# Six high and six low weight tiles, each at its own place in a 512-byte line

## The chip, the cores and the metric

The kernel runs on one core of a Trainium2 chip. The metric is the device time of one execution in microseconds (us); lower is better. A profile of one execution goes with it: its span runs from the first to the last instruction, and the execution's own time is a little longer.

## What is computed

A decoder trunk of two layers over 512 tokens of width 1024, in float32. Each layer is a half-step SwiGLU block, a mixer (a gated linear recurrence and a sliding-window attention side by side), and another half-step SwiGLU block:

```python
for l in range(DEPTH):                       # DEPTH = 2
    h = rms_norm(x, gn[0])
    x = x + 0.5 * rms_norm(swiglu(h, w_ffn1_gate[l], w_ffn1_up[l], w_ffn1_down[l]), gn[1])
    h = rms_norm(x, gn[2])
    proj = h @ w_in[l]                       # 1024 x 4864
    ...
    y_hg = hgrn2_mixer(hq, hf, hi, hg, ...) @ w_branch_hgrn[l]
    y_at = swa_sink_attention(aq, ak, av, attn_sinks[l]) @ w_branch_attn[l]
    mixed = sigmoid(gate_a) * y_hg + sigmoid(gate_b) * y_at
    x = x + rms_norm(mixed @ w_out[l], gn[3])
    h = rms_norm(x, gn[4])
    x = x + 0.5 * rms_norm(swiglu(h, w_ffn2_gate[l], w_ffn2_up[l], w_ffn2_down[l]), gn[5])
```

The feed-forward width is 2816. Nearly all of the arithmetic is in products of the 512 x 1024 activations with the weights, and each weight is used once.

## The kernel before

**Every product is done as three.** A float32 operand is kept as a pair: `hi`, its value rounded to the float32r type that the matrix engine takes in one pass, and `lo`, what the rounding left. `mm3` (L406) multiplies hi by hi, hi by lo and lo by hi into one accumulator. So three matmuls stand one behind the other: two with the high stationary operand, and one with the low one. The moving operand is 256 or 512 columns wide.

**The weight stream.** A weight unit is a tile of 128 partitions x 1024 columns, 4096 bytes in each partition. `load` (L235) brings it from HBM into one of four `w32` tiles. `split` (L322) and `quarter` (L255) make of it a high tile (`whi`, a rounding copy on ACT) and a low tile (`wlo`, a subtraction on DVE, or a negated copy on ACT to which a DMA issued by POOL adds the raw weight, L360). There are six tiles of each (`WS = 6`), used in turn. A consumer takes a tile in eight slices of 128 columns, which is 512 bytes of each partition.

**Who reads the tiles.** In the projections the weight slice is the stationary operand and the activations (tag `s`) move: the trace writes `acc<-s,whi` (output, moving, stationary). They are 512 wide in the mixer and in the first stages of a SwiGLU block, and 256 wide in `sevenths`, which makes the rest of gate and up with seven products in place of eight. In `down` it is the other way round: weight pieces move, 512 columns in four runs of 512 bytes, and activations are stationary (`acc<-whi,s`).

**What sets the order.** TensorE runs in the order in which the code is written; the other engines are ordered by a scheduler, with some steps pinned. A list of delays (`WAIT`) sets where the mixer's small steps are put between the matmuls.

**Where tiles lie.** All tiles of a tag are laid one behind the other in a partition, in the order in which tags first appear. As built, before the change, the starts of the tiles within a 512-byte line are these: all 61 `s` tiles at byte 64, all four `w32`, all six `whi` and all six `wlo` tiles at byte 128, `tt` and `m` (scratch of DVE and ACT) at byte 320, the identity matrix `ident` at byte 32, the matrix `ones` at byte 0. Tile sizes of these tags are multiples of 512 bytes, and so every slice of every such tile starts at the byte of its tag.

Of the kernel before, what the change touches and what calls it, by code (L numbers as in the profile page):

```python
# [8 lines left out]
F32R = mybir.dt.float32r  # L9
# [6 lines left out]
P = 128  # L16
D = 1024
# [19 lines left out]
W32, WS, AHEAD, TAIL, FIRST, EARLY, LATE = 4, 6, 3, 4, 7, 4, 8  # L37
# [7 lines left out]
def trunk(ctx: ExitStack, tc: tile.TileContext, xin, wall, gains, lbT, hgain, sinks, c_dist, c_mask, c_ident, out):  # L45
    nc = tc.nc
    cp = ctx.enter_context(tc.tile_pool(name="cp", bufs=1))
    sb = ctx.enter_context(tc.tile_pool(name="sb", bufs=1))
# [9 lines left out]
    def nm(s):  # L58
        seq[0] += 1
        return f"{s}_{seq[0]}"  # L60
# [3 lines left out]

    def small(shape, tag, bufs=4, dt=F32):
        return sb.tile(shape, dt, tag=tag, name=nm(tag), bufs=bufs)

    def acc():
        return ps.tile([P, S], F32, tag="acc", name=nm("acc"), bufs=5)
# [66 lines left out]
    eps_t = const([P, 1], "eps_t")  # L136
    nc.vector.memset(eps_t, EPS)
    nc.scalar.activation(out=small([P, 1], "warm", 2), in_=eps_t, func=AF.Copy, scale=eps_t)


# [15 lines left out]
    class Stream:  # L156
# [98 lines left out]
        def quarter(self, it):  # L255

            q, u, v, h = it.q, it.u, it.u + it.n, (slice(0, S), slice(S, D))

            def sums(o, x, y, op):
                for c in range(2):  # L260
                    pin(nc.vector.tensor_tensor(o[c], x[c], y[c], op=op))  # L261

            def raw(i):
                self.load(i + 1)
                return [self.raw[i][:, c] for c in h]

            def leave(i):
                self.raw.pop(i)
                self.freed += 1
                self.load(self.freed + W32)  # L270

            if it.kind in ("p1", "p2"):
                w = raw((u if it.kind == "p1" else v) + q)
            elif it.kind in ("p3", "p5"):
                w = self.b22[q]
            elif it.kind == "p7":

                w = self.b12[q]
                if q == 0:
                    sums(w, w, self.b22[q], ALU.add)  # L280
            else:
                w = self.b12[q]
            it.hi = sb.tile([P, D], F32R, tag="whi", name=nm("whi"), bufs=WS)
            it.lo = sb.tile([P, D], F32R, tag="wlo", name=nm("wlo"), bufs=WS)
            for c in range(2):
                i = nc.scalar.copy(it.hi[:, h[c]], w[c])  # L286
                if self.pinned:
                    pin(i)
            if it.kind == "p7" and q + 1 < it.n:
                sums(self.b12[q + 1], self.b12[q + 1], self.b22[q + 1], ALU.add)  # L290
            elif it.kind == "p6":
                sums(self.b22[q], self.b22[q], w, ALU.add)
            for c in range(2):
                pin(nc.vector.tensor_tensor(it.lo[:, h[c]], w[c], it.hi[:, h[c]].bitcast(F32), op=ALU.subtract))  # L294
            if it.kind == "p7":

                sums(w, raw(u + q), w, ALU.subtract)
                leave(u + q)
            elif it.kind == "p5":
                self.b22[q] = None  # L300
                if q + 1 < it.n:
                    sums(self.b12[q], raw(v + q), self.b12[q], ALU.add)
                    leave(v + q)
            elif it.kind == "p4":
                self.b12[q] = None
                if q == 0:
                    i = it.n - 1
                    sums(self.b12[i], raw(v + i), self.b12[i], ALU.add)
                    leave(v + i)
            self.done += 1  # L310
            self.flight += 1
# [10 lines left out]
        def split(self):  # L322
            it = self.items[self.done]
            if it.kind[0] == "p":
                return self.quarter(it)
            u, last = it.u, it.kind in "uvd"
            self.load(u + (1 if it.kind in "uv" else 2))
            it.hi = sb.tile([P, D], F32R, tag="whi", name=nm("whi"), bufs=WS)
            it.lo = sb.tile([P, D], F32R, tag="wlo", name=nm("wlo"), bufs=WS)
            w, h = self.raw[u], (slice(0, D // 2), slice(D // 2, D))  # L330
            cols = (slice(0, D),)
            if it.kind == "u" and u < 2:
                cols = h
            if it.kind in "bcd":
                v = self.raw[u + 1]
            if it.kind == "b":

                self.t13 = sb.tile([P, D], F32, tag="tt", name=nm("tt"), bufs=2)
                pin(nc.vector.tensor_tensor(self.t13[:, h[0]], w[:, h[0]], v[:, h[0]], op=ALU.add))
                pin(nc.vector.tensor_tensor(self.t13[:, h[1]], v[:, h[0]], v[:, h[1]], op=ALU.add))  # L340
                w = self.t13
                self.product()
            elif it.kind == "c":

                t = sb.tile([P, D], F32, tag="tt", name=nm("tt"), bufs=2)
                pin(nc.vector.tensor_tensor(t[:, h[0]], self.t13[:, h[0]], v[:, h[1]], op=ALU.add))
                pin(nc.vector.tensor_tensor(t[:, h[1]], t[:, h[0]], w[:, h[1]], op=ALU.add))  # L347
                w = t
            elif it.kind == "d":
                w = v  # L350
                cols = h[1:]
            for c in cols:
                i = nc.scalar.copy(it.hi[:, c], w[:, c])  # L353
                if u < 6 or self.pinned or self.tight:
                    pin(i)
                if it.kind in "vad":
                    i = nc.scalar.mul(it.lo[:, c], w[:, c], -1.0)  # L357
                    if self.pinned or self.tight:
                        pin(i)
                    nc.gpsimd.dma_start(it.lo[:, c].bitcast(F32), w[:, c], accum_op=ALU.add)  # L360
                else:
                    self.hold(nc.vector.tensor_tensor(it.lo[:, c], w[:, c], it.hi[:, c].bitcast(F32), op=ALU.subtract))  # L362
            self.done += 1
            self.flight += 1
            if last:
                nu = u + (1 if it.kind in "uv" else 2)
                for i in range(u, nu):
                    self.raw.pop(i)
                    self.freed += 1
                self.load(self.freed + W32)  # L370
# [93 lines left out]
    def rstd(sq, box, wait):  # L464


        n = sq.shape[-1] // P
        c = aux()
        for tt in range(n):
            mm(c[:, tt : tt + 1], sq[:, tt * P : (tt + 1) * P], ones[:, 0:1], True, True)  # L470
        rc = small([P, TT], "rc", 6)
        dg = big(F32, [P, TT, P])
        with tc.high_priority(offset=int(WAIT["first"])):
            nc.scalar.activation(out=rc[:, :n], in_=c[:, :n], func=AF.Sqrt, bias=eps_t, scale=1.0 / D)
            nc.vector.reciprocal(rc[:, :n], rc[:, :n])
            nc.vector.tensor_tensor(
                dg[:, :n, :], ident.unsqueeze(1).to_broadcast([P, n, P]),
                rc[:, :n].unsqueeze(2).to_broadcast([P, n, P]), op=ALU.mult,
            )
        yield WAIT[wait]  # L480
        b = aux()
        mm(b[:, : n * P], ones, dg[:, :n, :].rearrange("p a b -> p (a b)"), True, True)
        box.append(b)
# [15 lines left out]
    def pair_split(v, how=split):  # L499
        return how(v, to=(big(F32R, [P, 2, S // 2]), big(F32R, [P, 2, S // 2])))  # L500
# [139 lines left out]
    def root(ss, n):  # L640

        t = small([P, 2], "rt", 8)
        nc.vector.tensor_scalar(t[:, 0:1], ss[:, 0:1], 1.0 / n, EPS, op0=ALU.mult, op1=ALU.add)
        pin(nc.scalar.activation(out=t[:, 1:2], in_=ss[:, 1:2], func=AF.Sqrt, bias=t[:, 0:1], scale=1.0 / n))
        nc.vector.reciprocal(t[:, 1:2], t[:, 1:2])
        return t[:, 1:2]

    class Late:
# [20 lines left out]
        def first(self, k):  # L669
            x = big(F32R, [P, 2, S // 2])  # L670
            self.x1.append(split(self.src[k][:, HALF[0]], to=(x[:, 0, :], x[:, 1, :]), hold=pin))
# [973 lines left out]
```

## Time and profile before

| | |
|---|---|
| median of 3 runs | 2070.87 us (2067.01 to 2071.06) |
| the profiled execution's own time | 2067.36 us |
| its span | 2064.8 us |
| granted TensorE clock, mean | 0.999 |
| TensorE matmul busy | 2053.1 us, 99% |
| VectorE busy | 1629.0 us, 79% |
| ScalarE busy | 1249.3 us, 61% |
| GpSimd busy | 268.0 us, 13% |

Matmuls overlap: one begins before the one ahead of it has ended, and so its duration in the trace (276 ns for one of 256 columns) is longer than the distance to the next. What counts for the time is the distance from start to start, called cadence here. Where TensorE is busy without a break, the number of matmuls in a stretch gives it.

### The profile page before, as it was taken

How to read it: one execution, taken by the hardware profiler on the slowest of the kernel's cores; microseconds unless marked ns; L12 is line 12 of the kernel's file. 1: busy time of each engine (PE TensorE's matmuls, PEld its weight loads, DVE VectorE, ACT ScalarE, POOL GpSimd, SP SyncE). 2: the span in 40 equal slices, each digit the busy share in tenths (PEclk: the TensorE clock that was granted, in tenths of full speed). 3: DMA queues.
4: the chain of work that ended last, by engine and by line, in shares of the span. 5: the costliest groups of instructions: out<-in, count | busy, mean ns of one | idle time of the engine just before them, and what ended most of it. 6: DMA issues, size and time to landing. Idle time of an engine off the chain costs nothing. (4 is left out here: it accounts for less than half of the span.)

```text
span 2064.8 us, 36590 instructions
## 1 busy us (share of the span) xinstructions
PE 2053.1 (99%) x13571; PEld 1826.7 (88%) x13571; DVE 1629.0 (79%) x2910; ACT 1249.3 (61%) x2209; POOL 268.0 (13%) x318
## 2 busy tenths in 40 slices
PE   9999999999999999999999999999999999999999
PEld 8899978887888999997899998898778989999987
DVE  5887899666776778888988788977676758788888
ACT  7566687456355556658866666864653545666684
POOL 0111140000000011113201121400000100111140
PEclk9999999999999999999999999999999999999999
DMA  8587798312237367878758878872122562778794
GB/s 250 151 188 192 187 196 242 103 62 72 72 95 212 113 145 190 189 188 206 205 152 189 196 187 202 185 220 84 52 82 62 137 190 93 182 191 189 181 203 123
DMA packets 166802, 328.07 MB, mean 159 GB/s; under 512 B 19072, under 2 KB 85088, under 8 KB 166624
## 3 DMA queue, kind: packets, MB, share of 16 engines
q1 hardware_dynamic: 122416, 228.16, 33.1%
q0 software_dynamic: 44064, 97.54, 28.3%
q8 instruction: 106, 1.74, 0.3%
q14 instruction: 72, 0.59, 0.1%
q10 hardware_dynamic: 144, 0.05, 0.0%
HBM read 213.43 MB, written 14.73 MB: 110 GB/s over the span
## 5 line engine op out<-in xcount | busy, mean ns | idle before, releaser
L114 PE MATMUL acc<-s,whi 128*128 128x256 f32 (+1 forms) x4976 | 1031.0, 306 | 0.0
L114 PEld LDWEIGHTS acc<-s,whi 128*128 128x128 f32 x4976 | 793.8, 188 | 52.4 <-issue 3.2
L114 PE MATMUL acc<-s,wlo 128*128 128x256 f32 (+1 forms) x2488 | 759.9, 305 | 2.5 <-DMA wlo<-w 1.9
L114 PEld LDWEIGHTS acc<-s,wlo 128*128 128x128 f32 x2488 | 467.9, 188 | 30.7 <-DMA wlo<-w 4.4
L114 PE MATMUL acc<-whi,s 128*128 128x512 f32 x1360 | 446.6, 397 | 1.9 <-DVE s L432 1.3
L353 ACT CAST whi<-w 128x1024 fp32r<-128x1024 f32 (+1 forms) x310 | 286.8, 928 | 139.4 <-PE acc L114 90.0
L353 ACT CAST whi<-tt 128x1024 fp32r<-128x1024 f32 x160 | 167.9, 1049 | 252.3 <-DVE tt L347 171.4
L360 POOL DMA_DIRECT2D wlo<-w x178 | 154.2, 868 | 1249.5 <-ACT wlo L357 539.1
L114 PEld LDWEIGHTS acc<-whi,s 128*128 128x128 f32 x1360 | 255.7, 188 | 62.5 <-DVE s L432 2.2
L362 DVE TENSOR_TENSOR wlo<-tt,whi 128x1024 fp32r<-128x1024 f32 x160 | 196.0, 1225 | 135.7 <-ACT whi L353 129.8
L114 PE MATMUL acc<-wlo,s 128*128 128x512 f32 x680 | 267.6, 394 | 0.6 <-DVE wlo L294 0.6
L114 PE MATMUL aux<-s,whi 128*128 128x256 f32 (+1 forms) x1296 | 230.1, 280 | 0.0
L362 DVE TENSOR_TENSOR wlo<-w,whi 128x1024 fp32r<-128x1024 f32 (+1 forms) x132 | 157.5, 1204 | 78.7 <-ACT whi L353 77.8
L114 PEld LDWEIGHTS aux<-s,whi 128*128 128x128 f32 x1296 | 197.5, 188 | 1.1 <-issue 0.5
L114 PE MATMUL aux<-s,wlo 128*128 128x256 f32 (+1 forms) x648 | 181.0, 279 | 0.0
L114 PEld LDWEIGHTS acc<-wlo,s 128*128 128x128 f32 x680 | 128.0, 188 | 29.9 <-DVE wlo L294 2.4
L357 ACT ACTIVATE wlo<-w 128x1024 fp32r<-128x1024 f32 (+1 forms) x178 | 153.5, 863 | 0.2 <-PE acc L114 0.2
L114 PE MATMUL aux<-whi,s 128*128 128x512 f32 x432 | 145.3, 394 | 0.0
L443 POOL DMA_DIRECT2D s<-s x128 | 111.3, 969 | 217.5 <-ACT s L431 98.5
L114 PEld LDWEIGHTS aux<-s,wlo 128*128 128x128 f32 x648 | 121.6, 188 | 0.4
L294 DVE TENSOR_TENSOR wlo<-s,whi 128x512 fp32r<-128x512 f32 x160 | 102.5, 683 | 9.9 <-ACT whi L286 8.1
L431 ACT CAST s<-s 128x512 fp32r<-128x512 f32 (+1 forms) x140 | 70.6, 547 | 44.5 <-DVE s L490 41.0
(185 smaller groups left out, 2481.6 us busy)
## 6 DMA issues: line engine op xcount, KB each, us to landing
w<-wall SPq DMA_DIRECT2D x267, 512.0 KB, 4.1
wlo<-w POOLq DMA_DIRECT2D x98, 512.0 KB, 5.3
w<-wall SPq DMA_DIRECT2D x224, 128.0 KB, 3.5
wlo<-w POOLq DMA_DIRECT2D x80, 256.0 KB, 3.3
s<-wall SPq DMA_DIRECT2D x128, 128.0 KB, 4.4
s<-s POOLq DMA_DIRECT2D x64, 256.0 KB, 4.9
x_d<-s SPq DMA_DIRECT2D x48, 256.0 KB, 3.8
s<-x_d SPq DMA_DIRECT2D x48, 256.0 KB, 5.3
```

The costliest lines, as they stand in the source:

```text
L114: nc.tensor.matmul(o, lhsT, rhs, start=start, stop=stop)
L294: pin(nc.vector.tensor_tensor(it.lo[:, h[c]], w[c], it.hi[:, h[c]].bitcast(F32), op=ALU.subtract))
L353: i = nc.scalar.copy(it.hi[:, c], w[:, c])
L357: i = nc.scalar.mul(it.lo[:, c], w[:, c], -1.0)
L360: nc.gpsimd.dma_start(it.lo[:, c].bitcast(F32), w[:, c], accum_op=ALU.add)
L362: self.hold(nc.vector.tensor_tensor(it.lo[:, c], w[:, c], it.hi[:, c].bitcast(F32), op=ALU.subtract))
L431: (hold or ws.hold)(nc.scalar.copy(hi, src))
L443: nc.gpsimd.dma_start(lo.bitcast(F32), src, accum_op=ALU.add)
```

## The change

A helper `wtile` allocates the weight tiles 64 bytes longer than they are used, so each tile of a tag starts 64 bytes further in its 512-byte line than the one before. Ahead of the first low tile, a tile of 32 bytes is allocated, and so that it exists, GpSimd writes it once.

```diff
+    def wtile(tag):
+
+        return sb.tile([P, D + 16], F32R, tag=tag, name=nm(tag), bufs=WS)[:, :D]
...
-            it.hi = sb.tile([P, D], F32R, tag="whi", name=nm("whi"), bufs=WS)
-            it.lo = sb.tile([P, D], F32R, tag="wlo", name=nm("wlo"), bufs=WS)
+            it.hi = wtile("whi")
+            it.lo = wtile("wlo")
...
-            it.hi = sb.tile([P, D], F32R, tag="whi", name=nm("whi"), bufs=WS)
-            it.lo = sb.tile([P, D], F32R, tag="wlo", name=nm("wlo"), bufs=WS)
+            it.hi = wtile("whi")
+            if u == 0:
+                nc.gpsimd.memset(small([P, 8], "gap", 1), 0.0)
+            it.lo = wtile("wlo")
```

As built, the starts within a 512-byte line are now:

| tag | before | after |
|---|---|---|
| `whi`, six tiles | 128 each | 128, 192, 256, 320, 384, 448 |
| `wlo`, six tiles | 128 each | 32, 96, 160, 224, 288, 352 |
| `tt`, `m` | 320 | 96 |
| `s`, `w32`, `ident`, `ones` | 64, 128, 32, 0 | the same |

So high tiles still start at a multiple of 64 bytes, and low tiles now start 32 bytes off one. A low tile's offset from the activations, which was 64 bytes, is now between -32 and 288.

On all engines the instructions and their order are the same, but for one. On GpSimd, the program's first instructions were these (the names are those of tiles, with their numbers):

```order
L1635 MEMSET const-uint8-127 128x1
L1640 UNCONDITIONAL_BRANCH
L360 DMA wlo_381<-w_57_253 128x1024
L360 DMA wlo_434<-w_60_283 128x1024
L360 DMA wlo_500<-w_63_313 128x1024
```

And now they are:

```order
L1641 MEMSET const-uint8-127 128x1
L1646 UNCONDITIONAL_BRANCH
L334 MEMSET gap_137 128x8
L366 DMA wlo_383<-w_58_255 128x1024
L366 DMA wlo_436<-w_61_285 128x1024
```

A memset of eight columns stands ahead of GpSimd's first DMA; lines are six further down, and nothing else moved.

## The prediction

> **What bounds the kernel now.** I read the page's first part, then the waits of TensorE's two queues (matmuls and weight loads), then the number of matmuls by stretch.
>
> ```profile
> PE 2053.1 (99%) x13571; PEld 1826.7 (88%) x13571; DVE 1629.0 (79%) x2910; ACT 1249.3 (61%) x2209; POOL 268.0 (13%) x318
> ```
> ```profile
> PE acc L114 <- DMA wlo<-w: 1.9, 2, 1.2
> ...
> PEld acc L114 <- DMA wlo<-w: 4.4, 10, 1.4
> ```
>
> TensorE is busy 99% of the 2064.8 us, and its waits for any tile are a few us in all; the longest kind, for the DMA that completes a low tile, is 12 waits and 6.3 us. So nothing that DVE, ACT, POOL or a DMA gains or loses shows, unless it grows past the cover. What can move the time is the cadence of the matmuls themselves.
>
> The cadence isn't one number. These are the 256-wide stretches, by line L114 alone; the first column after the stretch is its length, and x after PE busy counts matmuls, some two of which began before the stretch:
>
> ```profile
> 90.00:230.00 140.00, 140.00 (x1236) 139.91 (x1235) 1.00 0.81 192
> ...
> 734.00:831.00 97.00, 96.84 (x844) 95.93 (x842) 1.00 0.79 187
> 831.00:841.00 10.00, 10.00 (x86) 10.00 (x85) 1.00 0.81 186
> 841.00:860.00 19.00, 19.00 (x170) 19.00 (x168) 1.00 0.79 186
> 861.00:900.00 39.00, 39.00 (x333) 38.94 (x331) 1.00 0.77 180
> ...
> 1069.00:1127.00 58.00, 57.16 (x502) 56.76 (x501) 1.00 0.77 180
> 1129.00:1256.00 127.00, 127.00 (x1081) 127.00 (x1080) 1.00 0.81 193
> 1757.00:1823.00 66.00, 65.88 (x578) 65.48 (x577) 1.00 0.78 182
> 1825.00:1942.00 117.00, 117.00 (x996) 117.00 (x995) 1.00 0.79 190
> ```
>
> 140 us by 1234 matmuls is 113.4 ns; 127 us by 1079 is 117.7 ns. The same code runs at two cadences, 4.3 ns apart (12.9 ns per group of three), with the clock granted in full (1.00) and the same DMA share. It isn't the neighbours' load either; the next rows, with all engines, have the same busy DVE and ACT in a fast and a slow stretch:
>
> ```profile
> 150.00:200.00 50.00, 50.00 (x444) 50.00 (x443) 40.77 (x59) 30.48 (x42) 9.48 (x11) 1.00 0.82 190
> 1140.00:1190.00 50.00, 50.00 (x427) 50.00 (x426) 40.76 (x59) 30.48 (x42) 9.43 (x11) 1.00 0.81 190
> ```
>
> The slow cadence begins behind a stall and stays until another. The timeline around 860 us (start, length, matmuls merged):
>
> ```profile
> 859.82 0.39 PE L114 MATMUL acc<-s,whi 128*128 128x256 f32 x2
> 860.30 0.39 PE L114 MATMUL acc<-s,wlo 128*128 128x256 f32 x1
> 860.53 0.40 PE L114 MATMUL acc<-s,whi 128*128 128x256 f32 x2
> ```
>
> Before it the stretch 841 to 860 is fast (170 in 19 us), behind it 861 to 900 is slow (333 in 39 us). A late low tile at 860.30 has shifted how weight loads and matmuls stand to each other, and the new standing holds for 39 us. So there is something inside TensorE that two streams, the moving operand and the next stationary one, share or step over, and in one standing it costs more. Whether the bytes at which they start matter is what the change asks, and before the change all tiles of a tag start at one byte, so this trace can't answer directly.
>
> The 512-wide products show two cadences too. These stretches are of `down`, 512 wide:
>
> ```profile
> 1260.00:1345.00 85.00, 85.00 (x366) 68.84 (x365) 1.00 0.84 194
> 968.00:1018.00 50.00, 50.00 (x221) 41.01 (x220) 1.00 0.82 206
> ```
>
> By 364 and 219 they are 233.5 and 228.3 ns. The slow one follows the slow 256-wide stretch that ends at 1256 us: the standing survives the change of width.
>
> **The change part by part.** *The memset* is 32 bytes wide on POOL, which is 13% busy, and stands ahead of its first DMA. The nearest row is a wider one:
>
> ```profile
> L1140 POOL MEMSET s<- x8: 306/308/640, 347.5 to 1510.9; 64x256 f32 x8
> L360 POOL DMA_DIRECT2D wlo<-w x178: 859/862/1157, 31.5 to 1933.5; - x178
> ```
>
> At most 0.64 us, done long before 31.5 us when that DMA is issued: nothing. Without that cover it would cost its 0.64 us once.
>
> *ACT and DVE* now write tiles at other bytes, and read `tt` at byte 96, not 320:
>
> ```profile
> L353 ACT CAST whi<-w 128x1024 fp32r<-128x1024 f32 x226 | 235.3, 1045 | 137.8 <-PE acc L114 90.0 <-DMA w<-wall 19.9 <-PE aux L114 19.0
> L353 ACT CAST whi<-tt 128x1024 fp32r<-128x1024 f32 x160 | 167.9, 1049 | 252.3 <-DVE tt L347 171.4 <-DVE tt L340 39.7 <-PE aux L114 28.6
> L362 DVE TENSOR_TENSOR wlo<-tt,whi 128x1024 fp32r<-128x1024 f32 x160 | 196.0, 1225 | 135.7 <-ACT whi L353 129.8 <-PE aux L114 3.5 <-PE acc L114 2.3
> L362 DVE TENSOR_TENSOR wlo<-w,whi 128x1024 fp32r<-128x1024 f32 x128 | 154.8, 1220 | 77.5 <-ACT whi L353 76.6 <-DMA half_ident<-c_ident 0.2
> ```
>
> A source at byte 128 (`w`) or 320 (`tt`) makes 4 or 5 ns of difference. Even 5 ns more or less on each of these 674 is 3.4 us spread over two engines that have 20% and 39% of the span free: I take nothing. If the free time were gone, those 3.4 us would be the bound, either way.
>
> *The DMAs into low tiles* land at other bytes as well. The nearest rows are those into low tiles at byte 128 and into `s` tiles at byte 64, both 256 KB:
>
> ```profile
> wlo<-w POOLq DMA_DIRECT2D x80, 256.0 KB, 3.3
> ...
> s<-s POOLq DMA_DIRECT2D x64, 256.0 KB, 4.9
> ```
>
> They differ by 1.6 us, of which an unknown part is other traffic. If each of the 12 waits above changed by that much, it would be 19 us of loss, or the whole 6.3 us of gain; the other DMAs have landed before they are asked for. Since their sizes and number stay, I take nothing and keep up to a few us for the range.
>
> *The matmuls* are the term that counts. Their numbers by shape:
>
> ```profile
> L114 PE MATMUL acc<-s,whi 128*128 128x256 f32 x3840 | 669.2, 278 | 0.0
> L114 PE MATMUL acc<-s,wlo 128*128 128x256 f32 x1920 | 535.5, 279 | 2.5 <-DMA wlo<-w 1.9
> L114 PE MATMUL aux<-s,whi 128*128 128x256 f32 x1280 | 224.6, 278 | 0.0
> L114 PE MATMUL aux<-s,wlo 128*128 128x256 f32 x640 | 177.8, 278 | 0.0
> ```
>
> There are 7680 of 256 columns, in 2560 groups of three. The slow stretches above make 10 + 39 + 127 + 117 = 293 us, and five short ones of 12 to 13 us are of the same kind (the second and the last of them):
>
> ```profile
> 709.00:722.00 13.00, 13.00 (x113) 13.00 (x112) 1.00 0.40 114
> ...
> 1732.00:1744.00 12.00, 12.00 (x104) 12.00 (x104) 1.00 0.40 96
> ```
>
> That is some 354 us, or 354 / 0.1177 = 3010 matmuls, at the slow cadence, and 4670 matmuls (1557 groups) at the fast one. Bounds from these rows: all at the fast cadence saves 3010 x 4.3 ns = 12.9 us; all at the slow one costs 4670 x 4.3 ns = 20.1 us. The 512-wide ones of `down` can move by 5.2 ns each between their two cadences. Most of them are in these two rows, 2040 matmuls, which bounds that at 10.6 us:
>
> ```profile
> L114 PE MATMUL acc<-whi,s 128*128 128x512 f32 x1360 | 446.6, 397 | 1.9 <-DVE s L432 1.3 <-ACT whi L286 0.6
> ...
> L114 PE MATMUL acc<-wlo,s 128*128 128x512 f32 x680 | 267.6, 394 | 0.6 <-DVE wlo L294 0.6
> ```
>
> Which way? A high slice still starts on a multiple of 64 bytes, only at another one; a low slice now starts halfway between two. The fast standing has been found with both streams starting on such multiples, and a group has one low slice among its three loads. I take it that the low load falls out of the fast standing and that each fast group pays half of what a slow group pays, since the two high loads keep it: 1557 x 6.45 ns = 10.0 us. Why half: one wholly slow group is 12.9 ns, none is 0, and no row is nearer to one end. On the profiled execution, 2067.36 + 10.0 = 2077.4 us; that execution is 3.5 us below the median of the runs shown, and on the median it is 2070.87 + 10.0 = 2080.9 us, which I forecast as 2081.
>
> The Trainium skill's "SBUF — State Buffer" (Door 1: The DMA port swizzle) gives SBUF lines of 16 bytes, with a penalty for an access that goes on to a new line. Both 64 and 32 are whole numbers of such lines, so by it a low slice touches as many lines as before and the 10 us would be 0. A row of the trace leans that way, for a slower kind of matmul:
>
> ```profile
> 2055.93 1.03 PE L124 MATMUL acc<-ident,s 128*128 128x128 f32 x8
> 2056.80 1.95 PE L114 MATMUL aux<-ones 128*128 128x128 f32 x16
> ```
>
> Eight transposes that read `ident` (byte 32, halfway) take 0.87 us from start to start, 109 ns each; the last one's own length is then 1.03 - 7 x 0.109 = 0.27 us. Sixteen that read `ones` (byte 0) take (1.95 - 0.27) / 15 us, 112 ns each. The halfway start isn't slower there. But these are not float32r, and take 109 ns for 128 columns where the weight products take 113 for 256, so the streams aren't pressed. This is why I don't put the price at its upper end.
>
> **The rivals.** *Faster: the stagger breaks the slow standing.* As tiles change every 24 matmuls, their bytes shift by 64, and a standing that costs more can't hold for 127 us. Then the slow stretches go: 12.9 us of the 256-wide ones. For it speaks that the slow standing is a lock that lives on regular starts, and the transposes above; against it, that each new tile is also a new chance to fall into it. 2070.87 - 12.9 = 2058 us. If 512-wide ones gain too, 5.2 ns each, some 1500 of them take it on to 2050. It decides from the point at which more than half of the slow 354 us are gone without a price on the low slices.
>
> *No change: bytes have no say.* The standing would come from when loads and matmuls start, not from where they read. For it speaks that DVE and ACT, which access other bytes all the time at 82% and 61% of the two 50 us stretches, leave each cadence untouched. Then only the stalls' luck differs: 2071 us, within some 3 us. The Trainium skill says this in the same page (Who interferes with whom): TensorE has two read ports of its own and never waits on anyone. The trace agrees as far as other engines go; the two cadences show that between its own two streams something does cost time.
>
> *Much slower: every group at the slow cadence or worse.* If staggered starts leave no cheap standing at all, the 4670 fast matmuls pay 4.3 ns each, 20.1 us, and the 2040 of `down` up to 10.6 us: 2102 us. Against it: the fast standing is found again and again behind other stalls, so it is not rare.
>
> **How the numbers follow.** A change of 0.2% (4 us) is about what a measurement of this kernel can tell from none. Chances: the forecast, slower by some 10 us, 0.36; faster, 0.36; no change, 0.19; much slower, 0.09. The forecast and the faster case stand level; I take the forecast because a price on the low slices needs only that the halfway start costs something, while the gain needs the stagger to help and the halfway start to be free. Its own range is 2075 to 2091 (0.0 to the upper bound of 20.1 us on the 256-wide ones). The range for 8 in 10 goes from 2050, the further end of the faster case, to 2096, between the forecast's upper end and the much slower case: 0.08 is left out below and 0.08 above. Faster by over 0.2%: 0.36 and a part of the no-change case, 0.37. Slower: 0.36 + 0.09 less what falls short of 4 us, 0.44. Same: 0.19.
>
> **What would show it.** In the profile after, matmuls per stretch in the 256-wide stages: some 436 in 50 us everywhere would be the forecast, 444 everywhere the faster rival, the same mix of 444 and 427 in long stretches no change, 427 or fewer everywhere the much slower one. ACT's 1045 ns and DVE's 1220 ns for 1024 columns should stay within 10 ns. The waits for low tiles' DMAs should stay near 6 us; if they grow by 10 us or more, my cause is wrong even where the sign is right. I'd be wrong altogether if cadences below 113 or 228 ns appeared.

## The result and the profile after

The changed kernel takes 2077.64 us (median of 4 runs, 2077.44 to 2078.25), the kernel before 2069.19 us in the same comparison (4 runs, 2067.01 to 2071.06). The ratio is 1.0045, with a 95% interval of 1.0033 to 1.0057: slower, by the medians some 8.5 us. The forecast was 2081 us and slower, with a range of 2050 to 2096.

The page of the changed kernel, first part: TensorE was the bound, and is so still more.

```profile
span 2075.7 us, 36592 instructions
...
PE 2069.6 (100%) x13571; PEld 1845.9 (89%) x13571; DVE 1630.6 (79%) x2910; ACT 1250.2 (60%) x2209; POOL 268.3 (13%) x319
```

The number of matmuls in three of the 256-wide stretches, line L118 alone (it was L114), in the form shown before:

```profile
100.00:150.00 50.00, 50.00 (x426) 1.00 0.79 187
...
1140.00:1190.00 50.00, 50.00 (x426) 1.00 0.81 191
...
1840.00:1890.00 50.00, 50.00 (x426) 1.00 0.80 190
```

Before, a stretch of 50 us held 444 matmuls or 427. Now it holds 426 in all of them: the fast cadence is gone. With two that began before the stretch, 50 us / 424 is 117.9 ns, 354 ns per group of three. The granted clock and the DMA share are what they were.

The other side of the sum is in the waits of TensorE's two queues, matmuls (PE) and weight loads (PEld): what was waited for, us in total, times, longest. First the kernel before, rows not shown so far:

```profile
PE acc L114 <- DVE s L432: 1.3, 2, 0.7
...
PE aux L114 <- DVE wlo L294: 0.6, 2, 0.3
...
PE acc L114 <- DVE wlo L294: 0.6, 2, 0.3
...
PEld acc L114 <- DVE wlo L294: 2.4, 7, 0.6
PEld acc L114 <- DVE s L432: 2.2, 2, 1.1
...
PEld aux L114 <- DVE wlo L294: 1.4, 3, 0.6
```

And the changed kernel: the only rows left in which TensorE waits for a low tile.

```profile
PEld acc L118 <- DVE wlo L368: 0.4, 1, 0.4
PEld acc L118 <- DMA wlo<-w: 0.2, 1, 0.2
```

On the queue of weight loads the DMA waits fall from 4.4 us to 0.2, those for DVE's low tiles of L294 from 3.8 us to none. A wait of both queues is counted in both, so rows of the two can't be added: the two DMA waits of the matmul queue before, 1.9 us, are at 1088.5 and 1128.1 us, where two of the ten waits of the weight loads are. So there were ten such waits and 4.4 us, and the 12 and 6.3 us of the prediction count two of them twice. The stalls are better measured in the spacing of the matmuls, which comes next.

**Where the 10.9 us of span come from.** Each matmul record was matched with its place in the program, and the distance from the first matmul of a group of three to the first of the next was taken. Groups longer than 384 ns (256 wide) or 768 ns (512 wide) are left out as stalled. Stalls are what the distance from one matmul to the next, where it is over 126 ns (256 wide), has above 118 ns, and one over 250 ns (512 wide, `down`) above 233 ns.

| | groups | before | after | difference |
|---|---|---|---|---|
| 256 wide, per group | 2560 | 345.6 ns | 353.8 ns | +21.0 us |
| 512 wide, projections | 576 | 699.9 ns | 695.9 ns | -2.3 us |
| 512 wide, `down` | 896 | 690.6 ns | 694.8 ns | +3.8 us |
| stalls, 256 wide and `down` | | 18.5 us | 7.8 us | -10.7 us |
| sum | | | | +11.8 us |

So 22.5 us were lost to the cadence and 10.7 us given back: a slower TensorE asks for each low tile later, and DVE and the DMAs are in time. Before, 1461 of the 2519 groups measured took about 340 ns and 1026 about 353 ns.

### The profile page after: what moved, and what is told of

Its sections match the earlier page's. It is cut to its first block, busy times and chain, and to the rows that moved or that the text cites. A ratio compares the mean times of both kernels' runs of the same rounds, so it can differ in the third digit from the quotient of the medians.

```text
span 2075.7 us, 36592 instructions
## 1 busy us (share of the span) xinstructions
PE 2069.6 (100%) x13571; PEld 1845.9 (89%) x13571; DVE 1630.6 (79%) x2910; ACT 1250.2 (60%) x2209; POOL 268.3 (13%) x319
## 4 chain that ended last, share of the span: by engine, by line
PE 99%; DMA 0%; DVE 0%; ACT 0%; issue 0%; ACTq 0%
PE acc L118 75%; PE aux L118 22%; PE aux L128 2%; PE acc L128 0%; DMA s<-xin 0%; DVE s L868 0%; ACT s L537 0%; ACT s L644 0%; DVE s L839 0%; DVE wlo L368 0%; ACT s L854 0%; DVE s L858 0%; ACT s L859 0%; ACT rt L650 0%; DVE rt L651 0%
## 5 line engine op out<-in xcount | busy, mean ns | idle before, releaser
L118 PE MATMUL acc<-s,whi 128*128 128x256 f32 (+1 forms) x4976 | 1044.7, 308 | 0.2 <-ACT whi L359 0.2
L118 PEld LDWEIGHTS acc<-s,whi 128*128 128x128 f32 x4976 | 798.0, 188 | 51.0 <-issue 3.2
L118 PE MATMUL acc<-s,wlo 128*128 128x256 f32 (+1 forms) x2488 | 762.5, 306 | 0.1
L118 PEld LDWEIGHTS acc<-s,wlo 128*128 128x128 f32 x2488 | 468.6, 188 | 26.1 <-DVE wlo L368 0.4
L118 PE MATMUL acc<-whi,s 128*128 128x512 f32 x1360 | 446.7, 397 | 0.0
L359 ACT CAST whi<-tt 128x1024 fp32r<-128x1024 f32 x160 | 167.9, 1049 | 255.2 <-DVE tt L353 190.0
L118 PEld LDWEIGHTS acc<-whi,s 128*128 128x128 f32 x1360 | 255.2, 188 | 63.5 <-issue 1.6
L118 PE MATMUL acc<-wlo,s 128*128 128x512 f32 x680 | 267.8, 394 | 0.0
L118 PE MATMUL aux<-s,whi 128*128 128x256 f32 (+1 forms) x1296 | 235.2, 282 | 0.0
L118 PEld LDWEIGHTS aux<-s,whi 128*128 128x128 f32 x1296 | 198.6, 188 | 1.1 <-issue 0.5
L118 PE MATMUL aux<-s,wlo 128*128 128x256 f32 (+1 forms) x648 | 182.5, 282 | 0.0
L118 PEld LDWEIGHTS acc<-wlo,s 128*128 128x128 f32 x680 | 127.8, 188 | 27.4
L118 PE MATMUL aux<-whi,s 128*128 128x512 f32 x432 | 145.5, 394 | 0.0
L118 PEld LDWEIGHTS aux<-s,wlo 128*128 128x128 f32 x648 | 122.1, 188 | 0.3
L290 ACT CAST whi<-s 128x512 fp32r<-128x512 f32 x160 | 90.1, 616 | 16.6 <-PE aux L118 10.5
```

The source lines that it names most:

```text
L118: nc.tensor.matmul(o, lhsT, rhs, start=start, stop=stop)
```

## The experiments

They ask first which part of the change costs, then what about a start byte does. Ratios are to the kernel before, on the same chip and in the same comparison; "offset" is a weight tile's start less that of the `s` tiles (byte 64, but for the last kernel), and cadences are worked out as above.

### The steps alone, and the 32 bytes alone

The first kernel keeps the steps of 64 bytes and has no gap of 32 bytes ahead of the low tiles.

```diff
-            it.hi = sb.tile([P, D], F32R, tag="whi", name=nm("whi"), bufs=WS)
-            it.lo = sb.tile([P, D], F32R, tag="wlo", name=nm("wlo"), bufs=WS)
+            it.hi = sb.tile([P, D + 16], F32R, tag="whi", name=nm("whi"), bufs=WS)[:, :D]
+            it.lo = sb.tile([P, D + 16], F32R, tag="wlo", name=nm("wlo"), bufs=WS)[:, :D]
```

> Only the 64-byte steps: high tiles start at bytes 128 to 448 of a 512-byte line, low tiles at 0 to 320, all on multiples of 64; no tile between them. Theory A (the forecast's: the low slices' halfway start is what costs): fast groups of three stay at 340 ns, the two cadences of before come back, time within 4 us of before (2069). Theory B (the steps from tile to tile break the fast standing): groups of 256-wide matmuls between 348 and 357 ns for most tile pairs as in the changed kernel, no long stretch at 340; time 6 to 10 us over before. Theory C (each offset between stationary and moving bytes has its own cadence): one value per tile pair, some at 340 and some at 353, time in between.

It took 2068.41 us, ratio 0.9997 (0.9987 to 1.0006): in time, the steps alone cost nothing that can be measured. (In cadence they do; the sum of all kernels below has it.) The second kernel has the gap and no steps: high tiles at byte 128, low tiles at byte 160.

```diff
             it.hi = sb.tile([P, D], F32R, tag="whi", name=nm("whi"), bufs=WS)
+            if u == 0:
+                nc.gpsimd.memset(small([P, 8], "gapb", 1), 0.0)
             it.lo = sb.tile([P, D], F32R, tag="wlo", name=nm("wlo"), bufs=WS)
```

> Only the 32 bytes: all high tiles at byte 128, all low tiles at byte 160. Theory A: each 256-wide group pays 6 to 13 ns, 346 to 353 ns throughout, time 8 to 20 us over before, less what stalls give back. Theory B: groups at 340 in long stretches, time within 4 us of before. Theory C: a constant cadence for the whole kernel that is not the one of before, either way.

It took 2084.07 us, ratio 1.0078 (1.0065 to 1.0090), 14.6 us over its kernel before. So it is the 32 bytes on the low tiles that make the time longer, and with the steps they cost less than alone. Two 256-wide stretches of each, steps first, then the 32 bytes:

```profile
100.00:150.00 50.00, 50.00 (x432) 1.00 0.78 188
...
1140.00:1190.00 50.00, 50.00 (x430) 1.00 0.80 195
```
```profile
100.00:150.00 50.00, 50.00 (x423) 1.00 0.78 183
...
1140.00:1190.00 50.00, 50.00 (x423) 1.00 0.80 196
```

With the steps, the stretch that had 444 lost and the one that had 427 gained: the long slow standing is broken, as the faster rival had it, but so is the long fast one. By pairs of tiles one sees what the 32 bytes add. Each row is one of the six pairs, its mean group of 256 wide:

| high tile at | steps alone: low at, ns | changed kernel: low at, ns | difference |
|---|---|---|---|
| 128 | 0, 340.9 | 32, 352.2 | +11.3 |
| 192 | 64, 354.7 | 96, 356.0 | +1.3 |
| 256 | 128, 349.9 | 160, 351.9 | +2.0 |
| 320 | 192, 357.9 | 224, 353.8 | -4.1 |
| 384 | 256, 341.9 | 288, 352.3 | +10.4 |
| 448 | 320, 354.3 | 352, 357.2 | +2.9 |

Two pairs of six are cheap with the steps alone, and they lie 256 bytes apart. The 32 bytes take just these two away.

### Is it the half, or the offset?

In the third kernel both low and high tiles start at byte 160: the gap of 32 bytes (`[P, 8]`) stands ahead of the high tiles instead, and nothing is stepped.

> High and low tiles all at byte 160: halfway against the activations at byte 64, without steps. Theory A, taken to its end: three of three loads start halfway, so groups at 353 ns or more and 20 us over before. Theory B: as before, 340 in long stretches. Theory C: one constant cadence per width, unknown before; if an offset of 96 bytes is free of clashes, at 340 or less everywhere and some 13 us under before.

It took 2090.29 us, ratio 1.0107 (1.0093 to 1.0121). In the fourth, the gap ahead of the high tiles is 448 bytes (`[P, 112]`), which puts both at byte 64, the byte of the activations: no start is halfway.

> All weight tiles at byte 64, the same as the activations, no steps. Theories A and B: nothing to pay, time within 4 us of before, the two cadences 340 and 353 as before. Theory C: another constant mix; if clashes are of equal places in a line, 353 or more everywhere and 15 to 25 us over before.

It took 2075.94 us, ratio 1.0040 (1.0027 to 1.0052): slower with no half in it. So "halfway" is not the whole rule. Its 256-wide and `down` stretches:

```profile
1140.00:1190.00 50.00, 50.00 (x419) 1.00 0.80 189
...
1290.00:1340.00 50.00, 50.00 (x222) 1.00 0.92 200
```

In 256 wide, 50 us hold 419, the slowest cadence of all (359.9 ns per group, the same in nearly every one). In `down`, 50 us hold 222, where the changed kernel held

```profile
1290.00:1340.00 50.00, 50.00 (x218) 1.00 0.93 201
```

that is 681.0 ns per group against 694.8: the cheapest of 512 wide. The byte that is worst for one width is best for the other.

### Offsets that are multiples of 64

Three kernels without any half and without steps. High at 128 and low at 0 (gap of `[P, 96]` between them), the pair that was cheap above:

> High tiles at byte 128 as before, low tiles all at byte 0, no steps. Theory A (the halfway start alone costs): no halfway start, so time within 4 us of before. Theory C (each offset has its own cadence): in the run with 64-byte steps, the tile pair at these two bytes held 340 ns per group of three with 256 columns throughout, so here all 2560 groups do, 2560 x 5.6 ns = 14 us under before, and some 2 us more or less on the 512-wide ones; stalls for low tiles give 2 to 5 us of it back.

2062.65 us, ratio 0.9972 (0.9962 to 0.9983), faster than before. The same with the high tiles 256 bytes on (gaps of `[P, 64]` ahead of them and `[P, 32]` between):

> High tiles at byte 384, 256 bytes further than before, low tiles at 0. Theory C with a period of 256 bytes: the same as with high at 128 and low at 0, groups at 340 ns. Theory C with a period of 512 bytes: another cadence, between 345 and 360. Theory A: as before.

2062.85 us, ratio 0.9975 (0.9964 to 0.9986); both have 340.6 ns per group, so 256 bytes on the high tiles make no difference. And the first with high and low exchanged, high at 0 and low at 128 (`[P, 96]` ahead, `[P, 32]` between):

> The offsets the other way round: high tiles at 0, low tiles at 128. Theory C if the distance between high and low is what counts: 340 ns as with 128 and 0. If each load's offset from the moving operand counts: not so, 353 or more, since two of three loads are now 64 bytes below the activations. Theory A: as before.

2079.57 us, ratio 1.0052 (1.0040 to 1.0064), 355.2 ns per group: the two tiles don't play the same part, and their distance from each other isn't what counts. One of its windows, then two windows of the first of the three, and that one's waits:

```profile
1140.00:1190.00 50.00, 50.00 (x423) 1.00 0.82 191
```
```profile
100.00:150.00 50.00, 50.00 (x444) 1.00 0.78 187
...
1140.00:1190.00 50.00, 50.00 (x443) 1.00 0.80 189
```
```profile
PE acc L114 <- DMA wlo<-w: 4.8, 6, 1.3
...
PEld acc L114 <- DMA wlo<-w: 9.1, 19, 1.5
```

The fast cadence now holds everywhere, but it was expected to bring more than 5.3 us: the waits for low tiles' DMAs, 1.9 and 4.4 us before, are 4.8 and 9.1. What the cadence gains, the stalls take in part.

### Thirty-two bytes on a cheap pair

The cleanest test of the 32 bytes: the cheap kernel (high 128, low 0), with the low tiles at 32 (gap of `[P, 104]` in place of `[P, 96]`).

> As in the run with high tiles at byte 128 and low tiles at byte 0 of the line (340.6 ns per group of three 256-wide matmuls, 2062.65 us), but all low tiles start at byte 32, and no tile is stepped: 32 bytes are the only difference. If it is the halfway start of the low slice that spoils a cheap pair, as the pair (128, 32) of the changed kernel suggests (352.2 ns), each of 2560 groups takes about 352 ns: +30 us of cadence over that run, less the stalls that a slower TensorE covers (28.7 us of them there, 6 to 8 in the slow kernels, so some 22 us back): 2068 to 2078 us, and 426 matmuls in 50 us. If the price in the changed kernel comes from tiles of different starts following each other, the cheap pair stays at 340 ns: 444 matmuls in 50 us, 2060 to 2065 us.

It took 2075.81 us, ratio 1.0033 (1.0020 to 1.0046), and 351.2 ns per group: the price of the pair (128, 32) in the changed kernel is its own and needs no steps. The same stretches:

```profile
100.00:150.00 50.00, 50.00 (x430) 1.00 0.78 187
...
1140.00:1190.00 50.00, 50.00 (x430) 1.00 0.80 192
```

And the 32 bytes on the high tiles instead, high at 160 and low at 0 (`[P, 8]` ahead, `[P, 88]` between):

> The same with the 32 bytes on the six high tiles instead: byte 160, low tiles at byte 0, nothing stepped. If a halfway start costs wherever it stands, two of the three loads of a group have it: at least as dear as with low tiles at byte 32, 352 ns or more per group, 2070 to 2090 us. If only the low slice's start counts (each group's third load), it stays at 340 to 342 ns and 2060 to 2066 us. If each pair of starts has its own cadence with no rule by halves, anything from 340 to 360 ns; then the two runs of this call need not stand in any order.

2078.44 us, ratio 1.0047 (1.0031 to 1.0064), 353.3 ns. Both loads count, and two halfway loads of three cost 2 ns more per group than one.

The Trainium skill's "SBUF — State Buffer" (Door 1: The DMA port swizzle) gives lines of 16 bytes, with a penalty for an access that goes on to a new one. What the prediction worked out from that, 32 bytes for nothing, doesn't agree with these runs: 10.6 ns per group, 27 us in 2560 groups, for a shift of two such lines.

### A place for each width

The last kernel gives each tile one of two places in a longer buffer, by the width of the product that reads it: in 256-wide stages the high tile at offset +64 and the low one at -64, elsewhere both at offset 0, all up to 256 bytes. The diff doesn't show the calls that mark an item as `narrow`. To make room, two constants move into a scratch tile, and the `s` tiles come to lie at byte 192.

```diff
+    def wtile(tag, it):
+        o = (0 if tag == "whi" else 32) if it.narrow else 48
+        return sb.tile([P, D + 64], F32R, tag=tag, name=nm(tag), bufs=WS)[:, o : o + D]
...
+            self.narrow = narrow or kind in "abcd"
...
-            it.hi = sb.tile([P, D], F32R, tag="whi", name=nm("whi"), bufs=WS)
-            it.lo = sb.tile([P, D], F32R, tag="wlo", name=nm("wlo"), bufs=WS)
+            it.hi, it.lo = wtile("whi", it), wtile("wlo", it)
```

> Each tile has 256 bytes more, and an item's slices start where its products want them: for 256-wide ones high at 64 and low at -64 bytes from the activations (modulo 256), for 512-wide ones both at the activations' own byte (modulo 256). Two small constants lie in scratch tiles to make room. Theory C with a period of 256 bytes: 340 ns per group of three of 256 columns and 680 of 512, which is 14 + 10 + 9 = 33 us under before less some us of stalls for low tiles, 2036 to 2045. With a period of 512 bytes: less than half of it. Theory A: as before.

It took 2054.28 us, ratio 0.9932 (0.9920 to 0.9944): the fastest of all, 13.6 us under its kernel before, though some 9 us short of what was expected. The cadences came as expected (340.6, 681.8 and 681.7 ns); but the stalls grew by 15.5 us, where some us were expected:

```profile
1140.00:1190.00 50.00, 50.00 (x444) 1.00 0.80 194
...
1290.00:1340.00 50.00, 50.00 (x222) 1.00 0.92 215
```
```profile
PE acc L118 <- DMA wlo<-w: 5.0, 7, 1.4
...
PEld acc L118 <- DMA wlo<-w: 8.7, 16, 1.6
PEld acc L118 <- DVE wlo L298: 6.4, 15, 0.6
```

This kernel also parts two readings of "start byte". Its 256-wide tiles lie, up to 256 bytes, at 0 (high) and 128 (low), exactly as in the kernel with 355.2 ns; but the activations lie at 192 instead of 64, and a group takes 340.6 ns. So it is the weight's start relative to that of the activations that sets the cadence, not the weight's byte alone.

### All kernels in one sum

Against before, in us: what the three cadences make (2560, 576 and 896 groups), what the stalls make, and their sum beside the measured difference of the profiled spans. Offsets are those of the high and low tiles from the activations, up to 256 bytes.

| offsets high / low | 256 wide, projections, `down`: ns per group | cadence | stalls | sum | span |
|---|---|---|---|---|---|
| +64 / +64 (before) | 345.6, 699.9, 690.6 | 0 | 0 | 0 | 0 |
| changed kernel | 353.8, 695.9, 694.8 | +22.5 | -10.7 | +11.8 | +10.9 |
| steps alone | 349.6, 696.6, 691.6 | +9.2 | -7.9 | +1.3 | +1.0 |
| +64 / +96 | 356.3, 693.8, 696.4 | +29.1 | -11.7 | +17.4 | +17.9 |
| +96 / +96 | 355.8, 702.8, 700.1 | +36.3 | -11.5 | +24.8 | +23.4 |
| 0 / 0 | 359.9, 681.6, 681.0 | +17.5 | -11.1 | +6.4 | +8.5 |
| +64 / -64 | 340.6, 695.4, 691.2 | -14.9 | +10.2 | -4.7 | -4.4 |
| +64 / -64, high 256 on | 340.6, 695.5, 691.3 | -14.7 | +12.2 | -2.5 | -2.3 |
| -64 / +64 | 355.2, 696.6, 693.4 | +25.2 | -11.6 | +13.6 | +13.0 |
| +64 / -32 | 351.2, 698.4, 699.6 | +21.5 | -10.9 | +10.6 | +10.0 |
| +96 / -64 | 353.3, 699.2, 693.5 | +21.9 | -11.2 | +10.7 | +11.0 |
| by width | 340.6, 681.8, 681.7 | -31.2 | +15.5 | -15.7 | -13.1 |

The sum meets the span within 2.6 us in every row. Wherever the cadence loses much, the stalls fall by 10 to 12 us and then no further; wherever it gains, 10 to 16 us of stalls come up. The row of before is one execution (2067.36 us) of a kernel whose runs beside the first experiments spread from 2064.44 to 2073.66 us, so another one would shift all differences by a few us.

Two other readings can be answered too. A gap moves more than what TensorE reads: the low tiles' DMAs land at other bytes, and the scratch tiles `tt` and `m` of DVE and ACT lie elsewhere. But as built, the kernels at +64 / -64 and +96 / -64 both have the low tiles at byte 0 and `tt` and `m` at byte 192, and still a group takes 340.6 ns in one and 353.3 in the other, with 10.2 us of stalls more and 11.2 us less. So the stalls follow the cadence, not the byte where a DMA lands.

And the row of the steps alone shows what their time hides. They lose 10.2 us of cadence in 256 wide (349.6 ns against 345.6) and gain 1.0 in 512 wide, and of the 9.2 us that are left fewer stalls cover 7.9.

## Why the prediction was right, and where not

**The bound.** Right: the cadence and the stalls of TensorE alone account for the span of the changed kernel and of all ten others within 2.6 us.

**Memset, ACT, DVE.** Right, they cost nothing. The rows of the changed kernel answer to those of before (1045, 1049, 1225 and 1220 ns):

```profile
L359 ACT CAST whi<-w 128x1024 fp32r<-128x1024 f32 x226 | 235.2, 1045 | 145.9 <-PE acc L118 98.5 <-PE aux L118 21.0 <-DMA w<-wall 16.5
L359 ACT CAST whi<-tt 128x1024 fp32r<-128x1024 f32 x160 | 167.9, 1049 | 255.2 <-DVE tt L353 190.0 <-DVE tt L346 35.6 <-PE acc L118 27.0
```
```profile
L368 DVE TENSOR_TENSOR wlo<-tt,whi 128x1024 fp32r<-128x1024 f32 x160 | 196.1, 1226 | 137.1 <-ACT whi L359 133.6 <-PE aux L118 3.5
L368 DVE TENSOR_TENSOR wlo<-w,whi 128x1024 fp32r<-128x1024 f32 x128 | 154.9, 1222 | 79.0 <-ACT whi L359 78.3 <-DMA w<-wall 0.4
```

**The halfway start of the low slice.** Right in sign, and as to what in the change costs time: the steps alone leave the time as it was (0.9997), the 32 bytes alone give 1.0078, and on a pair of cheap offsets they turn 340.6 ns into 351.2. But that loads on a multiple of 64 bytes keep the fast standing was wrong: with the steps alone, three of the six pairs have next to no group at 340 ns (their means are 354.3 to 357.9), and 256 wide loses 10.2 us, most of which fewer stalls hid. And as a rule it was too narrow: both tiles at the activations' byte, with no half anywhere, are dearer still in 256 wide (359.9 ns). The "regular starts" that the prediction credited with the fast standing are one of many offsets, and each offset has cadences of its own.

**The term, 1557 groups x 6.45 ns = 10.0 us.** Mis-sized. On the average each fast group paid the full difference, not half: the stretches hold 426, where 436 was forecast, and "427 or fewer everywhere" was the mark set for the much slower rival. In 256 wide the cost is 21.0 us against the 20.1 us that was named as the upper bound. The sum had no price for the steps: 10.2 us are theirs, and the 32 bytes add 10.8. That these are close to the forecast's 10.0 is luck, for without the steps the same 32 bytes cost 27.4 us. Taking the middle for want of a nearer row was the choice that failed; with that rival's price alone the 256-wide stages would have given 2091 us.

**The waits.** Forecast to stay near 6 us (4.4, counted once); they fell to 0.2 us. This is the step that failed unseen: the prediction asked only what a change in the transfers' own speed would do to the waits, and not what a slower TensorE does to them. The stalls gave back 10.7 us, almost exactly the half by which the term was too small. So it is luck that 2077.6 us lies near 2081: two errors of opposite sign nearly cancel, and the much slower rival, right on the cadence of 256 wide, missed the time by more.

**The rivals.** That bytes have no say is refuted by the time of every kernel but the one with steps alone, and by the cadences of that one's pairs, 340.9 to 357.9 ns. That the stagger breaks the slow standing is half true: it does, and breaks the fast one too, with nothing gained.

**Still open.** What in TensorE makes the offset matter is not shown, only that the starts of both streams enter, relative to each other. The period of 256 bytes was tried at few offsets. The transposes, by which the prediction argued that a halfway start can be free, were not tried at another byte. And the offset doesn't settle all: before, at one offset, groups of 340 and 353 ns stand in long stretches; and the pair at -64 / +64 took 355.2 ns where all tiles had it, 349.9 ns as one of six stepped pairs, with some 150 of its 391 groups at 340 ns.

## What to carry to other kernels

Where TensorE is busy without a break, count matmuls per stretch, and try where the stationary and the moving operand start relative to each other: a few hundred bytes of padding gave -0.7% here, the wrong ones +1.1%, and the best offset is not the same for 256 and 512 columns. And when a bound engine gets slower or faster, price its stalls again: those before it shrink or grow with it, and here they took back 32 to 86% of what the cadence did, in all eleven kernels and in both directions.

## What the runs showed of the hardware

In this kernel a float32r product's cadence depends on the start byte of its weight tile relative to that of its activations. With 256 columns a group of three takes 340.6 ns at +64 / -64 and 359.9 ns at 0 / 0, with 512 columns (`down`) 681.0 ns at 0 / 0 and 700.1 ns at +96 / +96, at a granted clock of 1.00 in every stretch shown. The Trainium skill's "SBUF — State Buffer" (Who interferes with whom) says that TensorE never waits on anyone; for other engines no run here speaks against that, but where its own two streams start relative to each other is worth up to 19 ns per group (359.9 against 340.6), which no row of waits reports.
